# A decoder trunk step on one core: 44 low-part subtractions of dense weights worked out by GpSimd in the odd mixer's first part

## The chip, the cores and the metric

The kernel runs on one core of a Trainium2 chip. Its engines are TensorE (PE; PEld is its weight load), VectorE (DVE), ScalarE (ACT), GpSimd (POOL) and SyncE (SP, which here only issues DMAs). The metric is the device time of one execution in microseconds (us); the median of three executions is given, and one more execution was profiled.

## What is computed

One inference step of a two-layer decoder trunk for 512 prompt tokens and 8 x 4 sample tokens (544 columns in all), with a model width of 1024:

```python
for l in range(DEPTH):                      # DEPTH = 2
    mod = (silu(c) @ ada_w[l] + ada_b[l]).reshape(bx, 3, 3, 1, D_MODEL)
    f = _swiglu(_modulate(x, mod[:, 0]), ffn_w_gate[l, 0], ffn_w_up[l, 0], ffn_w_down[l, 0])
    x = _layer_norm(ALPHA * x + 0.5 * (1.0 + mod[:, 0, 2]) * f, ln_g[l, 0], ln_b[l, 0])
    h = _modulate(x, mod[:, 1])
    m = even_mix(h) if l % 2 == 0 else odd_mix(h)
    x = _layer_norm(ALPHA * x + (1.0 + mod[:, 1, 2]) * m, ln_g[l, 1], ln_b[l, 1])
    f = _swiglu(_modulate(x, mod[:, 2]), ffn_w_gate[l, 1], ffn_w_up[l, 1], ffn_w_down[l, 1])
    x = _layer_norm(ALPHA * x + 0.5 * (1.0 + mod[:, 2, 2]) * f, ln_g[l, 2], ln_b[l, 2])
```

The odd mixer projects h to q, k, v of a dilated attention and to the inputs of RWKV-7 time mixing (`pd = h @ odd_w_in[..., 1536:]`), runs both, and projects their outputs back. RWKV-7 has 8 heads of 64; its state goes from token to token as `s = s*w - (s@kk) x (kk*a) + v x k`.

## The kernel before

**Dense products.** Activations lie with the model dimension on the partitions; a half is 272 of the 544 columns. Every float32 product is made of three float32r products on PE: a weight is split into a high part `wh` and a low part `wl`, an activation into `xh` and `xl`, and `mm3` (L456 to L462) adds wh·xh (L460), wh·xl (L461) and wl·xh (L462) in PSUM.

**Weights.** `tile512` (L442 to L450) makes one tile of 128x512 ready. SP loads it into `raw` (3 buffers), ACT copies it to `wh` (L448), and VectorE writes `wl = raw - wh` (L449), all in order on their queues. In the odd mixer `wh` and `wl` have 4 buffers each (`self.wide(4, 0)`). A strip is two such tiles and serves one block of 128 outputs: 8 steps for each of the two halves, so 48 matmuls, each tile read in both halves. `strip`, `piece` and `proj` call `tile512`.

**The odd mixer's first part** is the code in `odd_mix` from L1681 to L1721. It makes the two strips of the low-rank inputs (`rw_lora`), then the four strips of v (`vproj`), and then, for p = 0 to 3 (two heads each), the generator `rw_first(p)` with three strips (`xmix` of k, r and v), interleaved with `odd_qk(0)` to `odd_qk(2)` (two strips each), `rw_inverse(p)`, the recurrence `rw_rec(0)` and `rw_sample(p)`. `odd_qk(3)` comes later, in the second part. Most of the elementwise work of `rw_first` is VectorE's: L1387 to L1410 prepare k, kk and r, L1402 (`rKBf`) feeds the products of L1422, and L1440/L1441 are 62 small instructions, each of which needs the one before, that solve a triangular system in `rU` (`rEA` comes back through a DMA). L1367 is a scan over the decays. GpSimd makes border columns (L1300, L1301), keeps copies (L1317, L1318 `dsh`; L1448 `rRR`; L1457, L1458), makes small products for the sample (L1396 to L1411 `rSM`) and the diagonal `rMT` (L1449), each behind a wait for ACT or VectorE.

**Order.** The program is written in a rough order; the tile scheduler lays instructions out on each engine by its own estimate of times, and each engine then works strictly in that order. Whatever changes the estimate of one instruction can change the order around it on all engines.

Of the kernel before, what the change touches and what calls it, by code (L numbers as in the profile page):

```python
# [9 lines left out]
F32 = mybir.dt.float32  # L10
# [3 lines left out]
ALU = mybir.AluOpType  # L14
# [12 lines left out]
class Kern:  # L27
    def __init__(self, tc, D, es):
        self.tc, self.nc, self.D, self.es = tc, tc.nc, D, es
        self.n = 0  # L30
        pool = lambda n, b, **k: es.enter_context(tc.tile_pool(name=n, bufs=b, **k))
        self.cp = pool("const", 1)
        self.big = pool("big", 1)
        self.rawp = pool("raw", 3)
        self.sc2 = pool("sc2", 2)
        self.dr = pool("dr", 1, space=DRAM)
        self.banks = ExitStack()
        self.wes = ExitStack()
        self.psum(mm=4, ps=4)
        self.wide()  # L40
        self.xhl = self.xh, self.xl = [self.big.tile([128, 8, NT], F32R, name=n) for n in ("xh", "xl")]
        self.open_x()
# [399 lines left out]
    def tile512(self, src, room=None, lo=None):  # L442
        nc = self.nc
        w = src.shape[1]
        r = self.rawp.tile([128, 512], F32, name="raw")
        nc.sync.dma_start(r[:, 0:w], src)
        wh, wl = (room(n) if room else self.wp.tile([128, 512], F32R, name=n) for n in ("wh", "wl"))
        nc.scalar.activation(wh[:, 0:w], r[:, 0:w], AF.Copy)  # L448
        (lo or nc.vector).tensor_tensor(wl[:, 0:w], r[:, 0:w], wh[:, 0:w].bitcast(F32), op=ALU.subtract)  # L449
        return wh, wl  # L450

    def strip(self, src):
# [1217 lines left out]
    def odd_mix(self):  # L1670
        nc, D, tc = self.nc, self.D, self.tc
        es, ea = ExitStack(), ExitStack()
        pool = lambda n, b, e=es, **k: e.enter_context(tc.tile_pool(name=n, bufs=b, reuse_waits="tile", **k))
        self.wide(4, 0)
        self.psum(mm=2, ps=2, rs=2, rx=1, ro=1)
        self.rob = self.dr.tile([128, 2, SP], F32, name="rob")
        with es:
            pL, self.rg = pool("rkl", 1), pool("rg", 1)
            a1, r0 = pool("oa1", 1), pool("rr", 1)
            self.r0 = r0  # L1680
            self.rsm = pool("rsm", 1)  # L1681
            pA = pool("rk", 1, ea)
            self.rg2 = pool("rgb", 1, ea)
            pJ, p2 = pool("rkj", 1, ea), pool("rk2", 2, ea)
            self.omu = pA.tile([128, 14], F32, name="omu")
            nc.vector.tensor_scalar(self.omu, self.mu, -1.0, 1.0, op0=ALU.mult, op1=ALU.add)
            self.rw_setup(pL, pA, pool("rke", 9, ea), p2, pJ)
            pQ = pool("oqk", 1, side="right")
            self.rw_lora()
            early = {}  # L1690
            for s, k in zip(range(1), ('rx',)):
                src = D["odd_v"][s].rearrange("p k n -> p (k n)")
                w = [self.tile512(src[:, o:o + 512], lambda n: self.rp[0].tile([128, 512], F32R, name=n, tag="e"), None) for o in (0, 512)]
                early[s] = self.proj(None, 0, w, bank=lambda: self.bank[k].tile([128, 512], F32, name=k))
            self.f = {}
            f = [self.rw_first(p) for p in range(4)]
            self.vt = a1.tile([128, 5, 512], F32, name="vt")
            for _ in self.vproj(self.vt, D["odd_v"], self.E, lambda: self.bank["ro"].tile([128, 512], F32, name="ro"), early):
                pass
            nc.sync.dma_start(D["c_v"][0:512].rearrange("(t p) n -> p t n", p=128), self.vt[:, 0:4])  # L1700
            nc.sync.dma_start(D["c_v"][512:544], self.vt[0:32, 4])
            self.qs = a1.tile([128, 4, 32], F32, name="qs")
            self.ks = a1.tile([128, 4, 32], F32, name="ks")
            self.qk = {}
            next(f[0])
            next(f[0])
            for p in range(4):
                if p < 3:
                    next(f[p + 1])
                next(f[p], None)  # L1710
                if p < 3:
                    next(f[p + 1])
                for h in ((0,), (1,), (), (2,))[p]:
                    self.odd_qk(h, pQ)
                self.rw_inverse(p, *self.f[p])
                if p == 1:
                    self.rw_rec(0, r0, p2)
                if p < 3:
                    self.rw_sample(p)
            nc.sync.dma_start(D["d_shift"], self.dsh)  # L1720
            ea.close()  # L1721
            self.psum(mm=1, sc=4, sm=1, rx=1, ro=1)
            a1, pE, a2 = pool("oa3", 1), pool("rre", 2), pool("oa2", 2)
            for n, d in (("dmask", "dmask"), ("mold", "dmold"), ("smask", "dmnew")):
                setattr(self, n, self._ld(a1, d))
            self.qz = a1.tile([128, 3, 2, 128], F32, name="qz")
            nc.gpsimd.memset(self.qz, 0.0)
            pR = pool("ar2", 1)
            self.tmp = pool("art", 2)
            ada = self.ada([(1, 14), (1, 16)], lambda dt, tag: pR.tile([128, 512], dt, name="ar", tag=tag[0] + tag[2:]), lambda: self.bank["mm"].tile([128, 512], F32, name="mm"), 1)  # L1730
            self.rp = (pE, a2)
            self.aoT = a1.tile([128, 4, SP], F32, name="aoT")
            self.ro1 = a1.tile([128, 2, SP], F32, name="ro1")
            self.rw_rec(1, r0, a2)
            self.rw_sample(3, "sm")
            for h in (3,):
                self.odd_qk(h, a1)

            def units():
                for hp in range(4):  # L1740
                    for i in range(4):
                        yield self.odd_head(hp, i, a2)
                        if 4 * hp + i >= 8:
                            for _ in range(2):
                                next(ada, None)
                for _ in ada:
                    pass
            self.ahead(units())
            self.odd_sample(a1, a2)
            for hp in range(4):  # L1750
                self.split(self.xh[:, hp, 0:SP], self.xl[:, hp, 0:SP], self.aoT[:, hp])
            self.split(self.xh[:, 6:8, 0:SP], self.xl[:, 6:8, 0:SP], self.ro1)
            t = a1.tile([128, 2, SP], F32, name="rl", tag="sq")
            nc.sync.dma_start(t, self.rob)
            self.split(self.xh[:, 4:6, 0:SP], self.xl[:, 4:6, 0:SP], t)
            self.rw_sample_end()
        self.psum(mm=4, ps=4)
        self.wide()
# [261 lines left out]
```

## Time and profile before

| | |
|---|---|
| median of three executions | 2573.84 us (2569.62, 2573.84, 2588.95) |
| profiled execution | 2567.64 us, its span 2565.8 us, mean granted clock 0.969 |
| PE busy | 2442.6 us (95%), 20338 matmuls |
| PEld busy | 2253.4 us (88%) |
| DVE busy | 1232.4 us (48%), of these L449 `wl` 458.8 us in 664 |
| ACT busy | 943.3 us (37%), of these L448 `wh` 401.5 us in 664 |
| POOL busy | 409.0 us (16%) |
| chain that ended last, by engine | PE 82%, DVE 7%, DMA 4%, ACT 4%, issue 1%, POOL 1% |

Matmuls are pipelined, so PE's busy time says little about its rate. The granted clock is a share of full speed: 1.00 is 2.4 GHz and 0.50 is 1.2 GHz. The first part of the odd mixer lies between about 1646 and 1885 us of the span. The chain is followed back from the last instruction: at each step it goes to what released it, or to the instruction before it on its engine.

### The profile page before, as it was taken

To read this page: it belongs to the slowest core of one execution; us is meant where nothing else is said; L and a number is where in the kernel's file an instruction comes from. 1 tells how busy PE (TensorE), PEld (TensorE's weight loads), DVE (VectorE), ACT (ScalarE), POOL (GpSimd) and SP (SyncE) were. 2 spreads that over 40 slices of the span, in tenths; PEclk is the share of its full clock that TensorE was granted. 3 is DMA by queue.
4 is the path that set the end of the run, shared out by engine and by line. 5 is a ranking of instruction groups with operands and counts; after the bars stand their busy time and mean duration, and the time that the engine had idled before them with its cause. 6 is when DMAs were issued, how large, how long until landed. Compare 5 with 4: busy or idle time off the path is not lost.

```text
span 2565.8 us, 50682 instructions
## 1 busy us (share of the span) xinstructions
PE 2442.6 (95%) x20338; PEld 2253.4 (88%) x20338; DVE 1232.4 (48%) x2999; ACT 943.3 (37%) x2051; POOL 409.0 (16%) x616
## 2 busy tenths in 40 slices
PE   6999999899899999999999999889999999999996
PEld 4988999897588999999989999878877578999996
DVE  6532356544577333345423334558664567333343
ACT  4322323435555333224323322545422545333222
POOL 1000016411432000031000003312111122000032
PEclk8999999999999999999999999889988999999998
DMA  7666335567632222223562232322322632222221
GB/s 237 203 217 216 113 118 112 188 216 252 222 122 75 87 88 94 80 80 105 173 222 83 85 91 81 103 77 78 92 75 92 211 113 74 87 89 94 80 80 58
DMA packets 184027, 318.27 MB, mean 124 GB/s; under 512 B 38416, under 2 KB 47040, under 8 KB 183664
## 3 DMA queue, kind: packets, MB, share of 16 engines
q1 hardware_dynamic: 172096, 282.52, 34.6%
q0 software_dynamic: 10400, 31.06, 4.1%
q8 instruction: 159, 2.61, 0.4%
q10 hardware_dynamic: 1296, 1.46, 0.2%
q14 instruction: 76, 0.62, 0.1%
HBM read 288.68 MB, written 26.28 MB: 123 GB/s over the span
## 4 chain that ended last, share of the span: by engine, by line
PE 82%; DVE 7%; DMA 4%; ACT 4%; issue 1%; POOL 1%; SPq 1%; ACTq 0%; POOLq 0%; DVEq 0%
PE mm L460 23%; PE mm L462 23%; PE mm L461 22%; PE ps L185 2%; DVE x L347 1%; DMA ar<-in_ada_w 1%; DMA raw<-in_ada_w 1%; ACT t L249 1%; DVE wl L449 1%; PE sc L1178 1%; PE sc L1156 1%; PE ad L185 1%; PE ps L460 1%; PE ps L462 1%; PE ps L461 1%
## 5 line engine op out<-in xcount | busy, mean ns | idle before, releaser
L460 PE MATMUL mm<-xh,wh 128*128 128x272 f32 x3720 | 1089.4, 295 | 35.5 <-ACT xh L250 10.1
L461 PE MATMUL mm<-xl,wh 128*128 128x272 f32 x3720 | 1082.7, 291 | 2.0 <-DVE xl L251 2.0
L462 PE MATMUL mm<-xh,wl 128*128 128x272 f32 x3720 | 1083.0, 292 | 0.8 <-DVE wl L449 0.8
L460 PEld LDWEIGHTS mm<-xh,wh 128*128 128x128 f32 x3720 | 706.0, 190 | 85.2 <-ACT t L401 31.2
L449 DVE TENSOR_TENSOR wl<-raw,wh 128x512 fp32r<-128x512 f32 (+1 forms) x664 | 458.8, 703 | 537.0 <-ACT wh L448 505.0
L461 PEld LDWEIGHTS mm<-xl,wh 128*128 128x128 f32 x3720 | 710.5, 191 | 7.0 <-DVE xl L251 2.5
L462 PEld LDWEIGHTS mm<-xh,wl 128*128 128x128 f32 x3720 | 706.6, 190 | 7.8 <-issue 4.2
L448 ACT ACTIVATE wh<-raw 128x512 fp32r<-128x512 f32 (+1 forms) x664 | 401.5, 618 | 727.6 <-PE mm L461 565.9
L460 PE MATMUL mm<-hh,wh 128*128 128x272 f32 x1280 | 370.4, 289 | 0.0
L462 PE MATMUL mm<-hh,wl 128*128 128x272 f32 x1280 | 370.4, 289 | 0.0
L461 PE MATMUL mm<-hl,wh 128*128 128x272 f32 x1280 | 369.5, 289 | 0.0
L460 PEld LDWEIGHTS mm<-hh,wh 128*128 128x128 f32 x1280 | 241.4, 189 | 0.8 <-issue 0.4
L461 PEld LDWEIGHTS mm<-hl,wh 128*128 128x128 f32 x1280 | 241.2, 188 | 0.4
L462 PEld LDWEIGHTS mm<-hh,wl 128*128 128x128 f32 x1280 | 241.1, 188 | 0.4
L402 DVE TENSOR_TENSOR t<-t,mm 128x272 f32<-128x272 f32 x169 | 73.4, 434 | 279.6 <-ACT t L401 279.4
L401 ACT ACTIVATE t<-mm 128x272 f32<-128x272 f32 x169 | 65.6, 388 | 318.6 <-PE mm L462 318.6
L297 POOL TENSOR_TENSOR sa<-x 128x272 f32<-128x272 f32 x24 | 26.1, 1087 | 907.4 <-DVE x L291 852.0
L291 DVE SCALAR_TENSOR_TENSOR x<-mm,rg,x 128x272 f32<-128x272 f32 (+1 forms) x96 | 45.9, 479 | 171.4 <-PE mm L462 170.7
L466 DVE TENSOR_TENSOR hl<-t,hh 128x272 fp32r<-128x272 f32 x160 | 69.6, 439 | 35.8 <-ACT hh L465 35.3
L465 ACT ACTIVATE hh<-t 128x272 fp32r<-128x272 f32 x160 | 67.5, 426 | 38.5 <-DVE t L402 38.5
L277 POOL TENSOR_TENSOR sq<-sq,t 128x272 f32<-128x272 f32 x60 | 54.7, 926 | 18.1 <-ACT t L276 17.3
L249 ACT ACTIVATE t<-x,S,G 128x272 f32<-128x272 f32 (+1 forms) x80 | 44.5, 589 | 24.1 <-DVE x L348 23.5
(643 smaller groups left out, 2536.6 us busy)
## 6 DMA issues: line engine op xcount, KB each, us to landing
raw<-in_ada_w SPq DMA_DIRECT2D x192, 256.0 KB
raw<-in_wg SPq DMA_DIRECT2D x176, 256.0 KB
raw<-in_wu SPq DMA_DIRECT2D x176, 256.0 KB
raw<-in_wd SPq DMA_DIRECT2D x160, 256.0 KB
ar<-in_ada_w SPq DMA_DIRECT2D x96, 256.0 KB
raw<-in_odd_rw SPq DMA_DIRECT2D x28, 256.0 KB
xs<-x POOLq DMA_DIRECT2D x16, 272.0 KB, 4.0
x<-xs POOLq DMA_DIRECT2D x8, 544.0 KB, 7.8
```

The source lines that it names most:

```text
L185: return nc.tensor.matmul(ps[32 * j:32 * j + 32], self.c32[:, 9 * k:9 * k + 32], r, start=(k == 0), stop=(k == 7))
L249: nc.scalar.activation(t[:, 0:n], x[:, d, c0:pe], AF.Identity, scale=G[:, d, 0:1], bias=S[:, d, 0:1])
L277: G.tensor_tensor(s["q"], s["q"], t, op=A)
L401: self.act = nc.scalar.activation(s, pss[2 * i], AF.Silu)
L402: mul = nc.vector.tensor_tensor(s, s, pss[2 * i + 1], op=ALU.mult)
L448: nc.scalar.activation(wh[:, 0:w], r[:, 0:w], AF.Copy)
L449: (lo or nc.vector).tensor_tensor(wl[:, 0:w], r[:, 0:w], wh[:, 0:w].bitcast(F32), op=ALU.subtract)
L460: nc.tensor.matmul(ps, wh[:, s], mh, start=first, stop=False)
L461: nc.tensor.matmul(ps, wh[:, s], ml, start=False, stop=False)
L462: self.last = nc.tensor.matmul(ps, wl[:, s], mh, start=False, stop=last)
L465: self.nc.scalar.activation(hi, src, AF.Copy)
L466: return (lo_eng or self.nc.vector).tensor_tensor(lo, src, hi.bitcast(F32), op=ALU.subtract)
```

## The change

A field `self.lo` names the engine for the low parts when the caller names none. It is GpSimd from just behind `rw_lora()` to the end of the first part of `odd_mix`, and empty elsewhere. Strips made in between (4 of v, 12 of k, r and v of the time mixing, 6 of q and k: 22 strips, 44 tiles) get their `wl` from GpSimd.

```diff
+        self.lo = None
@@ tile512
-        (lo or nc.vector).tensor_tensor(wl[:, 0:w], r[:, 0:w], wh[:, 0:w].bitcast(F32), op=ALU.subtract)
+        (lo or self.lo or nc.vector).tensor_tensor(wl[:, 0:w], r[:, 0:w], wh[:, 0:w].bitcast(F32), op=ALU.subtract)
@@ odd_mix
             self.rw_lora()
+            self.lo = nc.gpsimd
@@ odd_mix
                 if p < 3:
                     self.rw_sample(p)
+            self.lo = None
             nc.sync.dma_start(D["d_shift"], self.dsh)
```

Lines of the changed kernel stand one to three further down (L449 is L450 there, L1402 is L1403). VectorE has 2957 instructions in place of 3001, GpSimd 665 in place of 621; the other engines have as many as before, in a partly different order from the odd mixer on.

VectorE, the end of `rw_first(0)`'s second piece (`rKBf` goes to PE's L1422; `e` are scratch rows of k and r). Before:

```order
L1397 TENSOR_TENSOR e<-e 128x544
L1398 TENSOR_TENSOR rKBf<-e 128x16x32
L1400 TENSOR_SCALAR e<-e,c_rw_par 128x544
L1406 SCALAR_TENSOR_TENSOR rSM<-rSM,rDC 128x32
L449 TENSOR_TENSOR wl<-raw,wh 128x512
L1401 SCALAR_TENSOR_TENSOR e<-e 128x544
L449 TENSOR_TENSOR wl<-raw,wh 128x512
L1402 TENSOR_TENSOR rKBf<-e 128x16x32
L1409 SCALAR_TENSOR_TENSOR e<-e,c_rw_par 128x544
```

The same place on VectorE now:

```order
L1398 TENSOR_TENSOR e<-e 128x544
L1399 TENSOR_TENSOR rKBf<-e 128x16x32
L1401 TENSOR_SCALAR e<-e,c_rw_par 128x544
L1407 SCALAR_TENSOR_TENSOR rSM<-rSM,rDC 128x32
L1402 SCALAR_TENSOR_TENSOR e<-e 128x544
L1403 TENSOR_TENSOR rKBf<-e 128x16x32
L1410 SCALAR_TENSOR_TENSOR e<-e,c_rw_par 128x544
```

The two subtractions are gone from between k's last steps. GpSimd, the same piece (`rSM` are the sample's small products, each waiting for a VectorE row above). Before:

```order
L1448 COPY rRR<-rQR 128x512
L1396 TENSOR_TENSOR rSM<-e 128x32
L1399 TENSOR_TENSOR rSM<-e 128x32
L1403 TENSOR_TENSOR rSM<-e 128x32
L1405 TENSOR_TENSOR rSM<-rSM,rDC 128x32
L1372 MEMSET e 128x16
```

GpSimd at that place now:

```order
L1449 COPY rRR<-rQR 128x512
L1397 TENSOR_TENSOR rSM<-e 128x32
L1400 TENSOR_TENSOR rSM<-e 128x32
L450 TENSOR_TENSOR wl<-raw,wh 128x512
L1404 TENSOR_TENSOR rSM<-e 128x32
L450 TENSOR_TENSOR wl<-raw,wh 128x512
L1406 TENSOR_TENSOR rSM<-rSM,rDC 128x32
L1373 MEMSET e 128x16
```

Both subtractions stand behind products that wait for VectorE; the second also behind L1404, which waits for VectorE's L1402. VectorE, the head of the triangular solve of p = 1 (the scan is p = 2's). Before:

```order
L1454 TENSOR_TENSOR rKBf<-rKBf,rDC 128x1024
L449 TENSOR_TENSOR wl<-raw,wh 128x512 x2
L1367 SCALAR_TENSOR_TENSOR e<-c_rscan,e 128x544
L1440 TENSOR_TENSOR rtm<-rU,rEA 128x31
L1441 TENSOR_TENSOR rU<-rU,rtm 128x31
```

Now the head is followed by the solve and a part of `rw_inverse(0)` (L1502), and the scan stands further down:

```order
L1441 TENSOR_TENSOR rtm<-rU,rEA 128x60
L1442 TENSOR_TENSOR rU<-rU,rtm 128x3x20
L1441 TENSOR_TENSOR rtm<-rU,rEA 128x76
L1502 TENSOR_TENSOR rVU<-rVU,rs 128x2x128
L1368 SCALAR_TENSOR_TENSOR e<-c_rscan,e 128x544
L1442 TENSOR_TENSOR rU<-rU,rtm 128x4x19
```

The scan of p = 2 moved behind the 13th product of the solve of p = 1.

## Rows read from the trace of the kernel before

**Rows 1.** Busy time by stretch: start:end, length, PE, PEld, DVE, ACT, POOL, granted clock, DMA.
```profile
1646.00:1690.00 44.00, 44.00 (x325) 42.33 (x324) 17.52 (x32) 23.59 (x50) 7.46 (x22) 0.95 0.36 119
1690.00:1730.00 40.00, 29.61 (x215) 26.62 (x214) 25.80 (x63) 17.83 (x31) 9.53 (x22) 0.74 0.20 58
1730.00:1790.00 60.00, 57.16 (x775) 52.68 (x773) 50.74 (x151) 31.85 (x67) 15.08 (x37) 1.00 0.29 81
1790.00:1840.00 50.00, 48.17 (x658) 42.09 (x657) 35.25 (x114) 21.49 (x47) 6.40 (x18) 0.97 0.36 99
1840.00:1885.00 45.00, 43.35 (x729) 36.31 (x731) 23.20 (x56) 12.36 (x30) 10.24 (x16) 0.97 0.18 56
```

**Rows 2.** Waits of PE, 1646 to 1885 us: total us, times, longest.
```profile
PE mm L460 <- ACT pdb L1310: 9.4, 4, 5.2
PE rs L1519 <- DVE rMT L1517: 3.1, 3, 1.6
PE ps L1422 <- DVE rKBf L1402: 2.0, 1, 2.0
PE rs L1528 <- DVE rRR L1526: 2.0, 2, 1.8
```

**Rows 3.** Line L449, 1646 to 1900 us: durations in ns (min/median/max); its waiters.
```profile
L449 DVE TENSOR_TENSOR wl<-raw,wh x44: 667/692/1126, 1647.7 to 1875.1; 128x512 fp32r<-128x512 f32 x44
...
  PEld rs L1615: 0.2, 1
```

**Rows 4.** Groups of instructions on DVE, 1690 to 1885 us: busy us, mean ns, idle before.
```profile
L449 DVE TENSOR_TENSOR wl<-raw,wh 128x512 fp32r<-128x512 f32 x30 | 21.1, 704 | 11.7 <-ACT wh L448 11.7
```

**Rows 5.** The chain that ended last: every piece of L449 in 1690 to 1885 us.
```profile
1706.72 0.71 DVE wl L449
...
1768.19 0.69 DVE wl L449
...
1782.94 0.67 DVE wl L449
...
1814.99 0.68 DVE wl L449
...
1817.62 0.69 DVE wl L449
```

**Rows 6.** Groups of instructions on POOL, 1646 to 1885 us, shapes apart.
```profile
L1449 POOL TENSOR_TENSOR rMT<-rid,rDC 128x1024 f32<-128x1024 f32 x4 | 7.6, 1901 | 14.2 <-PE rx L1544 14.1
L1644 POOL TENSOR_TENSOR rum<-rsw,c_rbmt 128x512 f32<-128x512 f32 x2 | 2.6, 1294 | 4.8 <-DVE rsw L1638 4.8
L1648 POOL TENSOR_TENSOR rS<-rS,rDC 128x512 f32<-128x512 f32 x2 | 2.1, 1044 | 6.9 <-PE rs L1633 6.9
```

**Rows 7.** Timeline of POOL at three places: start, us.
```profile
1717.71 1.90 POOL L1449 TENSOR_TENSOR rMT<-rid,rDC 128x1024 f32<-128x1024 f32 x1
...
1741.52 2.00 POOL L1411 TENSOR_TENSOR rSM<-e 128x32 f32<-128x32 f32 x1 [1.70 <-DVE e L1320]
...
1806.73 1.55 POOL L1644 TENSOR_TENSOR rum<-rsw,c_rbmt 128x512 f32<-128x512 f32 x1 [2.97 <-DVE rsw L1638]
```

**Rows 8.** Timeline of DVE at the same places, and the scan of p = 2.
```profile
1718.48 1.18 DVE L1440 TENSOR_TENSOR rtm<-rU,rEA 128x31 f32<-128x31 f32 x1 [3.13 <-DMA rEA<-rab]
...
1719.92 0.19 DVE L1440 TENSOR_TENSOR rtm<-rU,rEA 128x30 f32<-128x30 f32 x1
...
1758.51 1.29 DVE L1367 TENSOR_TENSOR_SCAN e<-c_rscan,e 128x544 f32<-128x544 f32 x1 [1.84 <-ACT e L1354]
...
1782.13 0.75 DVE L1395 TENSOR_TENSOR rQR<-e 128x512 f32<-128x512 f32 x1
...
1807.70 1.13 DVE L449 TENSOR_TENSOR wl<-raw,wh 128x512 fp32r<-128x512 f32 x1 [0.32 <-ACT wh L448]
```

**Rows 9.** Waits of ACT, 1646 to 1885 us: the longest in total.
```profile
ACT wh L448 <- PE mm L461: 46.5, 29, 9.9
```

**Rows 10.** Waits of SP's queue, 1646 to 1885 us: the longest in total.
```profile
SPq L446 <- DVE wl L449: 92.5, 26, 15.4
```

## Prediction

> **What bounds the kernel now.** I read the page first: PE is busy 95% of the span and holds 82% of the chain that ended last, so a VectorE instruction counts only where PE stands still. Next I split the mixer's first part into stretches [rows 1]. From 1646 to 1690 us PE has no idle time at all. From 1690 to 1885 it is idle 40 - 29.61 + 60 - 57.16 + 50 - 48.17 + 45 - 43.35 = 16.7 us of 195, most of it before 1730, where the granted clock also falls to a mean of 0.74 (PE runs part of that stretch at 1.2 GHz). VectorE is busy 25.80 + 50.74 + 35.25 + 23.20 = 135.0 us of those 195, and most densely from 1730 to 1790, with 50.74 of 60. GpSimd is busy under 50 us in all five stretches together.
>
> Then I asked what PE waits for there [rows 2]: 9.4 us for PSUM banks that ACT has not emptied, and 2 to 3.1 us each for three VectorE results (rMT, rKBf, rRR). A low part is not among them. The view of the line itself says the same: 44 subtractions with a median of 0.692 us, and only 0.2 us of PEld's waits are put down to them [rows 3]. So wl is always early, and its only way to the end is that it stands in VectorE's queue ahead of results that PE does wait for. The chain shows how often: 5 of the 30 that lie behind 1690 us are on it, with 0.71 + 0.69 + 0.67 + 0.68 + 0.69 = 3.4 us [rows 4, 5].
>
> **What goes.** 14 of the 44 lie before 1690 us, where PE is never idle: nothing to gain. The other 30 take 21.1 us off VectorE [rows 4], and 3.4 us off the chain [rows 5]: a sixth (3.4/21.1 = 0.16) of what is taken off the engine counts at the end.
>
> **What comes.** The trace has no subtraction of raw and wh on GpSimd, and no GpSimd result in float32r. The nearest rows are its float32 products of two 128x512 inputs: L1648 with 1.044 us, and L1644 with a mean of 1.294 [rows 6], one of which took 1.55 [rows 7]. I take 1.04 for one that is left alone, since shape and number of inputs agree, and keep 1.55 as the upper end. GpSimd gets 44 x 1.04 = 46 us of work (68 at the upper end) in 239 us, beside the 48.7 it has: 40 to 49% busy, so it does not become the bound.
>
> But the two engines get in each other's way. At 1717.71 GpSimd began the 1.90 us of L1449, up to 1719.61 [rows 7]; VectorE's L1440, which takes 0.19 us, began at 1718.48 and took 1.18, up to 1719.66 [rows 8]. VectorE stood until GpSimd had ended. At 1806.73 both had two inputs to read: L1644 took 1.55 in place of 1.04, and the VectorE subtraction behind took 1.13 in place of 0.69 [rows 7, 8]. At 1741.52 GpSimd waited instead: 2.00 us for a 128x32 product, under four VectorE instructions in a row [rows 7]. The Trainium skill (SBUF — State Buffer, Who interferes with whom) says that a VectorE instruction with two SBUF inputs and a GpSimd instruction that reads SBUF share one read interface, and that the second to come is blocked until the first ends; the first two places agree with it, with 1.18 us where 0.19 would do. It speaks against this change; what it would do is the first rival.
>
> So a subtraction on GpSimd is free for VectorE only where VectorE has nothing to do. Without wl, VectorE works 135.0 - 21.1 = 113.9 of 195 us, a share of 0.58. The 30 hold the inputs for 30 x 1.04 = 31.3 us; of these 0.58, or 18.3 us, fall on VectorE's other work and push it back. VectorE thus gets 21.1 - 18.3 = 2.8 us in all. Between the ends (no hold falls on it: 21.1 gained; all do: 31.3 - 21.1 = 10.2 lost) I take the share of busy time, since nothing aligns the two queues. At the end a sixth counts: 18.3 x 0.16 = 3.0 us come, 3.4 go, **net -0.4 us**.
>
> The Trainium skill (GPSIMD Engine Reference, Performance versus the Vector engine) gives GpSimd 1.96 times VectorE's time for such an addition. An estimate by it is 0.692 x 1.96 = 1.36 us for each, and the same sum then gives +0.4 us instead of -0.4; L1648's 1.044 us is only 1.5 times 0.692, and the sum goes by that.
>
> **Is wl late for PE?** By rows 1 a matmul of the stretch before 1690 takes 44.00/325 = 0.135 us, so a strip of 48 lasts 6.5 us. There are four buffers, two strips; the first tile of a strip is free after three quarters of it and is read again at the start of the strip after the next, 1.25 strips or 8.1 us later, and for the second tile it is the same. ACT's copy begins as soon as the buffer is free: it waits 46.5 us for exactly that [rows 9]. With a microsecond each for copy and subtraction some 6 us are left. On GpSimd the subtraction takes up to 0.9 us longer, and ahead of it may stand a 1.90 us L1449 or a product that waits for VectorE by a microsecond or two: 3 to 5 us at worst. I cost it at nothing; the cover is about 6 us, and a tile that used it all up would cost PE the rest. Behind a waiting L450 on GpSimd stand copies and sample products that PE does not wait for in these rows [rows 2]. SP's raw loads wait for wl (92.5 us in 26 waits [rows 10]) and would be issued up to 0.9 us later; the three raw buffers reach 1.5 strips ahead, 9.8 us, so this costs nothing either.
>
> **What else moves.** The scan of p = 2 stood in a gap of VectorE at 1758.51 and now stands behind the 13th product of a solve. It comes some 5 us later (12 pairs, each instruction 0.19 us [rows 8] or a little more); its results are first used on VectorE at 1782.13 [rows 8], 22 us behind its end, so the delay is covered, and the 1.29 us now lie in dense work: at most +1.3, by the sixth 0.2. The number of ACT's table loads is unchanged.
>
> **The rivals.**
> - **The lock decides (slower).** Where VectorE is densest, every hold falls on it, the two never fit together, and VectorE is the engine that PE waits for. Price: 10.2 us if all of the loss reaches the end, and 30 x 1.55 - 21.1 = 25 us if the holds are also 1.55 long. It turns slower once over 21.1/31.3 = 67% of the holds fall on VectorE work; from 1730 to 1790 its busy share is 85% now, and that speaks for it. Against it: PE has other work queued while VectorE is late, and only a sixth counted so far. Profiled time 2571 to 2578. This is also where the skill's rule leads if it holds without exception.
> - **VectorE's relief counts in full (faster).** The two subtractions at 1705 and 1706.72 go from in front of rKBf, for which PE waits 2.0 us [rows 2], in the stretch with the low clock. Then 3.4 us go and nothing comes back, a sixth of the 11.7 us that VectorE stood waiting for wh [rows 4] is 1.9 more, and if PE's clock stays up for a third of the stretch (29.61 x 0.26/3 = 2.6 us) it is 8 us: 2560. Against it: GpSimd's subtraction is ready at the same moment, and rKBf's inputs have to wait for it.
> - **Low parts come late for PE.** GpSimd's queue stands behind a wait while PE reaches the tile. Each such tile costs the lateness beyond 6 us; 30 tiles with 1 us each would be +30, 2598. No wait of GpSimd in the new order leads back to the strip itself, so I hold it unlikely.
> - That the change moves nothing is out: VectorE loses 44 instructions and GpSimd gains 44.
>
> **How the numbers follow.** The sum is 2567.64 - 0.4 = 2567.2 us for the profiled execution. The median of the three runs shown is 6.2 us above that execution; the two lower runs are 2.0 and 6.2 above it, 4.1 on average, and I add 4.1: **2571 us**. Chances: this sum, within 4 us either way, 0.50; the lock 0.24; full relief 0.20; late low parts 0.04; the rest, a changed order with an effect of its own, 0.02. The range goes from 2560 (full relief, 2560, which as a run lies 0 to 4 us above it) to 2585 (the lock's 10.2, 2578, with the median's 6.2), and leaves out late low parts, the longest holds and half of the extremes. A measurement of this kernel tells about 1% (26 us) from no change: faster 0.02, within 1% 0.93, slower 0.05.
>
> **What would show it.** Right: L450 at 1.04 to 1.6 us on GpSimd; PE's waits on L463 (wl) still under a microsecond; VectorE's busy time from 1690 to 1885 within some 5 us of before, since stretched instructions make up for the 30 that left; L1441 or L1442 with single rows of about 1.2 us beside a subtraction; the last L450 within 4 us of 1875 us, where the last moved subtraction starts now [rows 3]. Wrong: a subtraction of 2 us or more (the float32r result is slow there), PE waits on L463 of several us, or VectorE's solve stretched so that rMT or rRR waits of PE grow by 10 us.

## The result, and the profile after

The changed kernel takes 2599.76 us (median of six runs, 2592.95 to 2602.65) where the kernel before takes 2575.62 (six runs, 2569.62 to 2588.95). The two medians are 24 us apart. The ratio on record is an estimate of its own, not the quotient of these medians: 1.0070, with a 95% interval of 1.0052 to 1.0088, **some 18 us slower**, where 2571 and no change had been forecast. Two more comparisons of the same two kernels on other chips gave 1.0050 (1.0035 to 1.0066) and 1.0056 (1.0043 to 1.0070), some 13 and 14 us. The profiled execution took 2592.95 us, its span 2591.1, mean granted clock 0.964 (before 2567.64, 2565.8 and 0.969).

Not all of the 25 us between the two spans is the change's. Some 6 to 9 us arise at 640 to 720 us, in the even mixer, where the two programs are the same; the experiments below show such differences there between kernels with an equal program (560 to 720 us: granted clock 0.96 in one profile of the kernel before, 0.88 in another kernel that is no slower than it). The median of the kernel before is also not the same on every chip, 2568.9 to 2582.4. So runs are compared by their ratio to the kernel before on the same chip, and profiles by what PE does from a given matmul on.

The profile after, busy time by stretch, the columns as in [rows 1]:

```profile
1646.00:1690.00 44.00, 35.90 (x263) 34.26 (x263) 14.79 (x38) 23.38 (x52) 22.28 (x34) 0.92 0.36 119
1690.00:1730.00 40.00, 29.10 (x231) 25.23 (x230) 20.67 (x32) 22.26 (x40) 20.80 (x31) 0.84 0.32 98
1730.00:1790.00 60.00, 53.14 (x536) 49.22 (x536) 45.44 (x137) 25.17 (x55) 21.14 (x37) 0.88 0.23 63
1790.00:1840.00 50.00, 48.01 (x634) 42.65 (x635) 29.75 (x65) 19.86 (x43) 19.02 (x35) 0.97 0.33 95
1840.00:1885.00 45.00, 41.92 (x614) 36.54 (x612) 30.05 (x98) 20.81 (x45) 11.62 (x23) 0.92 0.20 54
```

The row to look at is 1730 to 1790: PE ran 775 matmuls there in [rows 1] and was busy for 57.16 us at a granted clock of 1.00. Now it gets 536 done, is busy for 53.14, and the clock has a mean of 0.88. (The first row begins earlier in the program than in [rows 1], because of the 9 us.) PE's waits behind 1690 us, from the waits of PE of 1646 to 1885 us (total us, times, longest), which answer [rows 2]:

```profile
PE rs L1520 <- DVE rMT L1518: 3.0, 1, 3.0
PE ps L1423 <- DVE rKBf L1403: 3.0, 1, 3.0
PE rs L1499 <- DVE rVU L1502: 2.0, 2, 1.5
...
PE ps L1471 <- DVE e L1463: 1.4, 1, 1.4
PE rs L1529 <- DVE rRR L1527: 1.1, 1, 1.1
PE rs L1515 <- DVE rVU L1502: 1.0, 2, 0.5
```

PE is idle for 22.8 us behind 1690 us, where it was 16.7. New are rVU (L1502, the subtraction of `rw_inverse`) and `e` (L1463), 4.4 us together. Of the old ones, rMT has a longer single wait, 3.0 where it was 1.6. The 3.0 of rKBf tells nothing: a second profile of the kernel before has 3.0 as well. The moved line itself, 1646 to 1900 us (durations in ns, min/median/max; no waiter is listed for it):

```profile
L450 POOL TENSOR_TENSOR wl<-raw,wh x44: 1259/1278/1752, 1656.7 to 1899.4; 128x512 fp32r<-128x512 f32 x44
```

### The profile page after: what moved, and what is told of

Same layout as the page of the kernel before. It is cut to its first block, busy times and chain, and to the rows that moved or that the text cites. A ratio compares the mean times of both kernels' runs of the same rounds, so it can differ in the third digit from the quotient of the medians.

```text
span 2591.1 us, 50665 instructions
## 1 busy us (share of the span) xinstructions
PE 2458.6 (95%) x20338; PEld 2262.1 (87%) x20338; DVE 1223.9 (47%) x2955; ACT 943.6 (36%) x2051; POOL 457.2 (18%) x660
## 5 line engine op out<-in xcount | busy, mean ns | idle before, releaser
L450 DVE TENSOR_TENSOR wl<-raw,wh 128x512 fp32r<-128x512 f32 x620 | 427.5, 702 | 514.1 <-ACT wh L449 480.1
L449 ACT ACTIVATE wh<-raw 128x512 fp32r<-128x512 f32 (+1 forms) x664 | 401.3, 618 | 722.7 <-PE mm L462 554.1
L450 POOL TENSOR_TENSOR wl<-raw,wh 128x512 fp32r<-128x512 f32 x44 | 57.5, 1313 | 88.0 <-ACT wh L449 78.9
```

Of the source, the lines that this page charges most:

```text
L450: (lo or self.lo or nc.vector).tensor_tensor(wl[:, 0:w], r[:, 0:w], wh[:, 0:w].bitcast(F32), op=ALU.subtract)
```

## Experiments

Two causes are possible. **The hold**: GpSimd's subtractions delay VectorE. **The order**: the scheduler laid the instructions of all engines out differently. Issue-order edges tell them apart. They fix which instruction of an engine is issued ahead of which, and add no wait between engines. A kernel with such edges carries a table of places in the written program, and behind the program:

```python
def pin(nc, tc):
    ins = list(nc.cur_bb.bb.instructions)
    for steps in json.loads(zlib.decompress(base64.b85decode(ORDER))):   # one list per engine
        at = steps[0]
        for d in steps[1:]:
            tc.add_manual_dep(ins[at + d], ins[at].name, DependencyInfo(NoSync, DATA), reason="order")
            at += d
```

"Old order" means that every instruction but the 44 low parts stands on its engine as in the kernel before; "new order", as in the changed kernel. The places of the 44 themselves are the scheduler's in either. "Zeros" is the run that writes zeros in place of the subtraction.

### Hold and order, each alone

`pool_oldorder` is the changed kernel in the old order:

```diff
         with ExitStack() as es:
             Kern(tc, D, es).run()
+        pin(nc, tc)        # ORDER: the order before the change
```

> The changed kernel (44 low parts on GpSimd), with every engine's other instructions pinned by issue-order edges to the order that they had before the change; only the place of the 44 in GpSimd's queue is the scheduler's. Theory A (the new order costs the time: the scan of p = 2 and rw_inverse(0) changed places): ratio to before 0.998 to 1.002, since the order that costs is gone; profiled span near 2566. Theory B (the hold: GpSimd's 1.28 us subtractions push VectorE's dense chains back and lower PE's clock): the loss stays, ratio 1.005 to 1.009, L1441 rows of 1.2 us beside subtractions. Theory C (most of the difference is execution to execution, the first 9 us of it in the even mixer): ratio 1.000 to 1.004, and the lag against before at 720 us of the span anywhere from 0 to 9.

Measured: 1.0041 (1.0027 to 1.0055), 10.5 us. **The hold alone costs 0.4%.**

`dve_neworder` is the kernel before with the same two lines, and ORDER from the changed kernel:

> The kernel before (all low parts on VectorE), with every engine's other instructions pinned to the order of the changed kernel. Theory A (order): slower like the changed kernel, ratio 1.005 to 1.009, and VectorE stands some 9 us for rEA at about 1776 us. Theory B (hold): no loss, ratio 0.998 to 1.002. If order and hold each cost a part, this one and the run with the old order share the 18 us between them.

Measured: 1.0050 (1.0036 to 1.0064), 12.9 us. **The order alone costs 0.5%**, without one low part moved. Neither theory is out; each alone is nearly as slow as the changed kernel.

`pool_memset` writes zeros in place of the subtraction, in the old order:

```diff
-        (lo or self.lo or nc.vector).tensor_tensor(wl[:, 0:w], r[:, 0:w], wh[:, 0:w].bitcast(F32), op=ALU.subtract)
+        self.lo.memset(wl[:, 0:w].bitcast(F32), 0.0) if self.lo else (lo or nc.vector).tensor_tensor(...)
```

> Old order pinned, and in place of each of the 44 subtractions GpSimd writes zeros to the same tile of 128x512: the low part of these weights is left out of the result. VectorE is relieved of 44 instructions, GpSimd has as many, but they read no SBUF. Theory B (the hold by reading): faster than or equal to before, 0.995 to 1.000 (3.4 us of the chain gone, nothing back), and no L1441 row of 1.2 us beside a memset. Theory A: the same, 0.998 to 1.000, since the order is the old one. If it is as slow as the changed kernel, neither the reading nor the order is the cause but GpSimd's writes or the missing VectorE rows themselves.

Measured: 0.9998 (0.9989 to 1.0007). VectorE is busy for 1206.1 us in place of 1232.4, and no gain is seen. **The loss does not come with the move as such, but with what a subtraction does and zeros don't**: it reads, and takes longer. A relief of less than 2.8 us (0.11%) would not show in this ratio, and the profiles speak for one. From the first matmul of L1353 (L1354 here) to the end of the span the kernel before takes 906.5 and 905.2 us in its two profiles, and this one 902.4 in its only one. That is 2.8 to 4.1 us less, about the 3.4 that were forecast to go. So the relief is small, and whether it is nothing or some 3 us stays open.

`before_again` is the kernel before, profiled once more.

> The kernel before, unchanged, profiled once more. Theory C: its span differs from 2565.8 us by up to 9 us, and part of it lies at 665 to 705 us, in the even mixer, where the program is the same in all kernels here. Theories A and B: within 3 us of 2565.8, and no shift at 665 to 705 us.

Its span was 2565.3 us, 0.5 from the first, with up to 4.1 us between the two on the way (at 701 us). The row of busy time by stretch of this kernel in the even mixer and, on another chip, of `pool_off_solve` (below), which is no slower than the kernel before:

```profile
560.00:720.00 160.00, 152.13 (x1132) 109.07 (x1133) 79.06 (x256) 86.38 (x210) 47.07 (x79) 0.96 0.69 219
```

```profile
560.00:720.00 160.00, 151.16 (x1065) 109.14 (x1064) 72.40 (x229) 73.41 (x181) 39.58 (x70) 0.88 0.66 212
```

In equal programs PE has 67 matmuls fewer done here, at a clock of 0.88 in place of 0.96. That part of the 25 us is not the change's.

### What a hold looks like

The old order makes rows comparable one by one. Timeline of VectorE under zeros (start, us, [idle before]):

```profile
1729.65 0.72 DVE L1388 TENSOR_TENSOR e<-e 128x544 f32<-128x544 f32 x1 [1.39 <-ACT e L1386]
1730.29 0.22 DVE L1442 TENSOR_TENSOR rU<-rU,rtm 128x68 f32<-128x68 f32 x1
1730.43 0.72 DVE L1389 SCALAR_TENSOR_TENSOR e<-e 128x544 f32<-128x544 f32 x1
```

The same three in `pool_oldorder`:

```profile
1732.02 0.73 DVE L1388 TENSOR_TENSOR e<-e 128x544 f32<-128x544 f32 x1 [1.39 <-ACT e L1386]
1732.66 1.30 DVE L1442 TENSOR_TENSOR rU<-rU,rtm 128x68 f32<-128x68 f32 x1
1733.89 1.82 DVE L1389 SCALAR_TENSOR_TENSOR e<-e 128x544 f32<-128x544 f32 x1
```

and GpSimd's timeline beside them:

```profile
1732.59 2.54 POOL L450 TENSOR_TENSOR wl<-raw,wh 128x512 fp32r<-128x512 f32 x2 [7.82 <-ACT wh L449]
```

L1442 begins just behind the first of two subtractions and ends as it ends (1732.66 + 1.30 = 1733.96, the subtraction 1732.59 + 2.54/2 = 1733.86); L1389 begins beside the second and ends 0.6 us behind it (1735.71 and 1735.13). VectorE loses 2.2 us at this place. The sum over the kernel is in VectorE's busy time on the page, with the same 2955 instructions each time. Zeros, then whole subtractions:

```profile
PE 2445.8 (95%) x20338; PEld 2254.5 (88%) x20338; DVE 1206.1 (47%) x2955; ACT 943.5 (37%) x2051; POOL 424.4 (17%) x660
```

```profile
PE 2448.4 (95%) x20338; PEld 2256.7 (88%) x20338; DVE 1223.1 (47%) x2955; ACT 944.2 (37%) x2051; POOL 459.2 (18%) x660
```

1223.1 - 1206.1 = **17.0 us of holds**; GpSimd's subtractions are 58 us long together, so 29% of their time comes back as longer VectorE work. The Trainium skill (SBUF — State Buffer, Who interferes with whom) says that the second to come on the shared read interface is blocked until the first ends; the rows at 1732.66 agree with it, and the zeros, which read nothing, hold nobody here: no VectorE row of L1442 is longer than 0.28 us under zeros, and the longest in `pool_oldorder` has 1.31. Nor does any wait of PE or VectorE from 1690 to 1890 us in `pool_oldorder` end with a result of GpSimd, so it is not GpSimd's own results that come too late.

### Where a hold counts

`pool_on_solve` gives GpSimd only the 20 low parts that stood beside the triangular solves, `pool_off_solve` only the other 24, both in the old order:

```diff
+        self.nlo += bool(self.lo)
-        (lo or self.lo or nc.vector).tensor_tensor(wl[:, 0:w], ...)
+        (lo or self.lo if 18 < self.nlo <= 38 else nc.vector).tensor_tensor(wl[:, 0:w], ...)
```

> Old order pinned; only the 20 low parts (19th to 38th) that GpSimd worked out beside the triangular solves (1732 to 1839 us in the run with the old order) are GpSimd's, the other 24 VectorE's. If what counts is a hold in the solve, where each instruction needs the one before: all of the 0.4% stays, 1.0035 to 1.0045. If every hold counts alike: 20 of 44, 1.0015 to 1.0025.

> The complement: the 24 low parts away from the solves on GpSimd, the 20 beside them on VectorE, old order pinned. If holds count in the solve alone: 0.999 to 1.001. If every hold counts alike: 1.002 to 1.003. If relief is worth anything outside the solves, below 0.999, and this one would be faster than both kernels.

Measured: 1.0038 (1.0022 to 1.0054) beside the solves, 0.9997 (0.9983 to 1.0011) away from them. **The hold's cost comes from the 20 beside the solves; the other 24 cost nothing that is seen.** Nor is a gain seen from them, though one of less than 4.4 us would not show in this ratio; by the count above (from L1354 to the end of the span) the profile of the 24 has 903.5 us, 1.7 to 3.0 less than the kernel before. VectorE's busy time says the same of the holds. Each low part that leaves VectorE takes (1232.4 - 1206.1)/44 = 0.60 us off it (less than its own 0.69, since neighbours overlap). Without holds it would be 1232.4 - 20 x 0.60 = 1220.4 and 1232.4 - 24 x 0.60 = 1218.0; it is 1235.2 and 1218.9, so 14.8 us of holds beside the solves and 0.9 elsewhere. The waits of PE from the second L1423 of p = 1 on, 1766 to 1860 us. `pool_off_solve`:

```profile
PE rs L1520 <- DVE rMT L1518: 2.2, 2, 2.0
PE rs L1529 <- DVE rRR L1527: 2.0, 2, 1.8
```

`pool_on_solve`:

```profile
PE rs L1499 <- DVE rVU L1502: 5.0, 1, 5.0
PE rs L1520 <- DVE rMT L1518: 3.6, 2, 3.4
PE rs L1529 <- DVE rRR L1527: 2.1, 1, 2.1
```

The 5.0 us are a chain. The timeline of VectorE in `pool_off_solve` and then in `pool_on_solve`:

```profile
1778.68 0.20 DVE L1441 TENSOR_TENSOR rtm<-rU,rEA 128x31 f32<-128x31 f32 x1 [3.39 <-DMA rEA<-rab]
...
1780.86 0.41 DVE L1502 TENSOR_TENSOR rVU<-rVU,rs 128x256 f32<-128x256 f32 x1
```

```profile
1782.37 0.19 DVE L1441 TENSOR_TENSOR rtm<-rU,rEA 128x31 f32<-128x31 f32 x1 [6.83 <-DMA rEA<-rab]
...
1786.57 0.41 DVE L1502 TENSOR_TENSOR rVU<-rVU,rs 128x256 f32<-128x256 f32 x1
```

The holds in the solve of p = 0 make rMQ late, with it the transfer that brings rEA, and so the head of the solve of p = 1, for which VectorE stands 6.83 us in place of 3.39. Counted from the L1423 at 1766 us, the head is 3.5 us later; 2.0 of them are there when SP issues the transfer (1775.28 and 1773.10), the rest is added while the transfer runs, which no hold explains. Behind that head, ten instructions further, L1502 is queued, for which PE waits. Between head and L1502 two more holds of a microsecond follow (4.20 us in place of 2.18). Then the clock goes. Busy time by stretch from the same matmul on, 20 us each, `pool_off_solve`:

```profile
1766.30:1786.30 20.00, 20.00 (x206) 17.69 (x206) 12.54 (x41) 13.11 (x26) 1.91 (x9) 1.00 0.46 117
1786.30:1806.30 20.00, 17.57 (x341) 16.14 (x340) 18.56 (x60) 9.85 (x21) 4.09 (x10) 1.00 0.10 32
1806.30:1826.30 20.00, 20.00 (x262) 17.29 (x262) 13.36 (x31) 5.07 (x14) 5.15 (x9) 1.00 0.43 106
```

and `pool_on_solve`:

```profile
1766.49:1786.49 20.00, 15.52 (x149) 13.47 (x149) 9.35 (x27) 11.91 (x23) 6.49 (x11) 0.94 0.45 111
1786.49:1806.49 20.00, 19.45 (x307) 18.35 (x308) 15.86 (x53) 8.44 (x17) 3.59 (x7) 0.80 0.08 27
1806.49:1826.49 20.00, 17.91 (x275) 15.91 (x276) 13.88 (x41) 5.96 (x15) 7.91 (x16) 0.88 0.34 85
```

PE is idle 4.48 us in the first stretch, 0 in the other kernel. In the second, when it is busy again, the granted clock has a mean of 0.80 in place of 1.00: 20 x 0.20 = up to 4.0 us at full speed, on top of the wait. Stretches of 10 us of `pool_on_solve` show that the clock is back at 1.00 before it falls once more (PE alone: busy, granted clock, DMA):

```profile
1790.00:1800.00 10.00, 10.00 (x151) 0.78 0.01 2
1800.00:1810.00 10.00, 8.10 (x150) 1.00 0.19 55
1810.00:1820.00 10.00, 9.81 (x117) 0.83 0.13 21
```

The second fall, which makes the 0.88 of the third stretch, stands behind the wait of 2.1 us for rRR at 1808 and comes only after the clock had recovered from the first; in `pool_off_solve` a wait of 1.8 us for rRR leaves the clock at 1.00.

`pool_both`: VectorE keeps its 44 and GpSimd reads as well (old order).

```diff
-        (lo or self.lo or nc.vector).tensor_tensor(wl[:, 0:w], ...)
+        (lo or nc.vector).tensor_tensor(wl[:, 0:w], ...); self.lo and self.lo.tensor_tensor(self.dup, wh..., wh..., op=ALU.subtract)
```

> Old order pinned, VectorE keeps its 44 low parts, and GpSimd in addition subtracts wh from itself into a scratch tile 44 times (bf16 result, read by nobody): the hold without the relief. The runs so far say that the relief is worth nothing (zeros from GpSimd: ratio 0.9998) and the hold 0.4% (old order: 1.0041). If that holds, the ratio is 1.004 again, and VectorE has some 20 instructions of 1.2 us where 0.2 would do. If relief is worth the 3.4 us that the chain showed, this one is slower than the old order by that: 1.0055. If the hold needs the wait for a result of GpSimd, 1.000.

Measured: 1.0056 (1.0034 to 1.0078). The hold needs no result of GpSimd. Against 1.0041 the intervals overlap, so this run can't say what the relief is worth.

### Shorter holds

`pool_copy` lets GpSimd copy raw (one input); `pool_halves` works each low part out in two halves of 256 columns; both in the old order.

```diff
-        (lo or self.lo or nc.vector).tensor_tensor(wl[:, 0:w], ...)
+        self.lo.tensor_copy(wl[:, 0:w], r[:, 0:w]) if self.lo else (lo or nc.vector).tensor_tensor(wl[:, 0:w], ...)
```

```diff
-        (lo or self.lo or nc.vector).tensor_tensor(wl[:, 0:w], ...)
+        [(lo or self.lo or nc.vector).tensor_tensor(wl[:, a:z], ...) for a, z in (((0, 256), (256, w)) if self.lo else ((0, w),))]
```

> Old order pinned; GpSimd copies raw to the low part's tile (one input of 128x512 in place of two; the low part of these weights is wrong by that, and counts as the weight itself). If any GpSimd instruction that reads SBUF holds VectorE's two-input instructions: rows of L1441 and L1442 as long as what is left of the copy, and a loss in proportion to its length; 1.002 to 1.004 if it takes 0.5 to 1.3 us. If only a two-input instruction holds: 1.000, as with the zeros.

> Old order pinned, 44 low parts on GpSimd, each worked out in two halves of 256 columns: 88 instructions of about 0.65 us. A VectorE instruction is then held for half as long, but twice as often. If the total of the holds decides: 1.003 to 1.005, as with whole tiles (1.0041 and 18 us stretched). If single long holds decide, as the one-input copy of 0.61 us suggests (4.9 us stretched, ratio 0.9994): 0.999 to 1.002.

| in the old order | one on GpSimd, median | VectorE busy | holds | ratio to before |
|---|---|---|---|---|
| zeros, 44 | 0.526 us | 1206.1 | 0 | 0.9998 (0.9989 to 1.0007) |
| copy, 44 | 0.612 us | 1211.5 | 5.4 | 0.9994 (0.9982 to 1.0006) |
| halves, 88 | 0.734 us | 1220.9 | 14.8 | 1.0028 (1.0014 to 1.0041) |
| whole, 44 | 1.282 us | 1223.1 | 17.0 | 1.0041 (1.0027 to 1.0055) |

(Holds are VectorE's busy time less that under zeros.) No cost is seen for 5.4 us; 14.8 cost 7, 17.0 cost 10.5, each net of what the relief is worth. Two halves are longer than one whole (1.47 us) and stretch more of VectorE's rows, each by less, so their total is hardly smaller. Whether single length or total decides is not told apart by this. The cost is hardly proportional to the total (5.4 us would then cost 3.3, and the interval of the copies ends at 1.5), but three points whose intervals in part overlap give no more than that.

### What in the order costs

`pool_lora_first` is the changed kernel with five edges in place of the table: on PE, ACT and VectorE p = 2's decays (L1354, their sigmoids, the scan) ahead of rw_inverse(0).

```diff
+EDGES = ((17154, 16930), (17156, 16950), (17155, 16938), (17157, 16958), (17158, 16939))
```

> The changed kernel with five issue-order edges only: on PE, ACT and VectorE the decays of p = 2 (the products of L1354, their sigmoids, the scan of L1368) stand ahead of rw_inverse(0)'s instructions, as before the change; all else is the scheduler's. If the order's cost (12.9 us, ratio 1.0050 with the low parts on VectorE) comes from p = 2 starting behind rw_inverse(0): ratio about 1.004, as with the whole old order pinned. If it lies in the rest of the new order: 1.007, as the changed kernel.

Measured: 1.0075 (1.0053 to 1.0096). My first theory of the order, that p = 2's decays start too late, gains nothing from it. It isn't a clean test: with these decays ahead ACT has one ACT_TABLE_LOAD more (1.28 us; 2052 instructions on the page in place of 2051), in this kernel and in the four below that share its order of the decays. Three runs followed on one chip: the same order with the low parts on VectorE, the changed kernel once more, and the new order with four steps of rw_inverse(0) later on PE. The edit of the last, in PE's list (mm3 are dense matmuls):

```diff
 mm3 x37
+L1353 x2, mm3 x14
 L1498 x16
-L1353 x2, mm3 x14
+L1353 x2, mm3 x14
 L1498 x16
-L1353 x2, mm3 x14
+mm3 x24
 L1514 x32
-mm3 x24
+mm3 x20
 L1519 x32
-mm3 x20
```

> All low parts on VectorE, every engine's other instructions pinned to the order of the run with the five edges (decays of p = 2 ahead of rw_inverse(0); with the low parts on GpSimd it was 1.0075). If that order is no better than the changed kernel's: 1.003 to 1.006, and PE waits of 1 to 3 us at 1760 to 1785 us with a granted clock under 1 behind them. If that order is as good as the old one and GpSimd's holds alone made its 1.0075: 0.999 to 1.001.

> The changed kernel, unchanged, beside the others on one chip. Ratio again 1.005 to 1.009; the two parts measured alone (hold 1.0041, order 1.0050) add up to 1.009, so 1.007 would say that they share a part of their waits.

> All low parts on VectorE, the changed kernel's order pinned, but on PE four steps of rw_inverse(0) (both groups of L1498, L1514, L1519) stand one piece of 14 to 24 dense matmuls later each. If the order costs because PE reaches these steps before rTT and rMT are there (1.61 and 3.13 us of waits at 1761 and 1779) and its clock falls behind the waits (0.69 and 0.83 in the two stretches of 10 us), both are gone: 1.000 to 1.002. If the order costs by something else (the later p = 2 itself): still 1.004 to 1.006.

Measured: 1.0060 (1.0042 to 1.0077), 1.0050 (1.0035 to 1.0066) and 1.0041 (1.0027 to 1.0055). The covered steps no longer wait, but PE then waits 2.3 us for ACT's decays, 1.9 for pdb and 1.9 for L1382: the waits have moved. Then the scan was put into VectorE's wait for rEA: with the low parts on VectorE by VectorE's list, and with them on GpSimd by its edge, which now leads to the head of the solve (five edges again, where the expectation says six).

```diff
 L1454
+L1367
 L1440, L1441: the first 11 of the solve of p = 1
-L1367
```

```diff
-(17158, 16939)
+(17158, 17241)
```

The third is the first of these two with the old order as VectorE's list:

```diff
-ORDER = [PE, DVE, ACT, POOL, SP] of dve_scan_gap
+ORDER = [PE, ACT, POOL, SP] of dve_scan_gap, [DVE] of the kernel before
```

> As the run with that order and the low parts on VectorE (1.0060), but the scan of p = 2 stands ahead of the first product of the solve of p = 1, in the 5.3 us that VectorE stood there for rEA, in place of behind its 11th. If the order costs because the scan lies inside the solve (1.28 us in the solve, and all of p = 2 five to seven us later): most of the loss goes, 1.000 to 1.003. If it lies elsewhere in the new order: 1.005 to 1.007 again.

> The changed kernel (44 low parts on GpSimd, the scheduler's own order) with six issue-order edges: the decays of p = 2 ahead of rw_inverse(0) on PE, ACT and VectorE, and the scan ahead of the solve of p = 1. If the scan's place is what the order costs: as the old order with GpSimd's holds, 1.003 to 1.005. If not: 1.006 to 1.008, as with five edges (1.0075).

> PE, ACT, GpSimd and SP in the order of the run before (scan of p = 2 in the gap, 1.0051), the low parts on VectorE, but VectorE's other instructions in the order before the change. There rw_inverse(0)'s four subtractions stand behind the 10th, 11th, 19th and 22nd instruction of the solve of p = 1 (18th, 19th, 36th and 39th in the run before), its two rMT behind the 35th (50th, 51st), and p = 2's elementwise steps between the 36th and 50th (51st to the end). If VectorE's order is what the new order costs: 1.000 to 1.002, and PE's waits of 1.50 and 2.15 us at 1786 to 1794 us are gone. If it is the order of the matmuls: 1.004 to 1.006 again.

Measured: 1.0051 (1.0033 to 1.0068), 1.0043 (1.0031 to 1.0055) and 1.0067 (1.0053 to 1.0081). With the low parts on GpSimd, the scan in its gap gives what was expected if the scan's place were all that the order costs: 1.0043 in place of 1.0075 on another chip, no more than the hold alone. With them on VectorE it gives what was expected if the cost lies elsewhere: 1.0051 in place of 1.0060, with no hold of GpSimd to explain the rest. So the scan's place can be a part of the cost, and it isn't all of it; nor does VectorE's old order alone bring the time back. What these orders have in common is seen in the 50 us from the second L1422 (L1423) of p = 1 on, the row of busy time by stretch. The kernel before, `before_again`:

```profile
1751.23:1801.23 50.00, 47.57 (x701) 42.31 (x702) 37.30 (x116) 25.90 (x55) 7.92 (x25) 1.00 0.32 82
```

`dve_neworder`, then `dve_scan_gap`, then `dve_old_vector`:

```profile
1755.00:1805.00 50.00, 44.98 (x579) 40.59 (x580) 34.03 (x105) 22.33 (x47) 5.88 (x19) 0.90 0.28 72
```

```profile
1770.20:1820.20 50.00, 45.68 (x632) 41.07 (x636) 33.90 (x107) 24.95 (x50) 6.59 (x20) 0.93 0.31 79
```

```profile
1753.61:1803.61 50.00, 44.62 (x581) 40.70 (x581) 34.93 (x115) 24.39 (x49) 6.28 (x20) 0.93 0.23 57
```

The old order keeps PE busy for 47.57 us at a clock of 1.00 and gets 701 matmuls done. Each of the three other orders shown has 1.9 to 3 us more of idle time and a clock of 0.90 to 0.93, and 69 to 122 matmuls fewer. Where PE waits differs each time: rTT (1.6) and rMT (3.1) in `dve_neworder`, rVU (1.5) and L1514 (2.2) in `dve_scan_gap`, rVU (2.6) and rRR (2.8) in `dve_old_vector`. That the waits go with the order is shown; **which row of the new order starts them is not settled**, and with the low parts on VectorE the old order is the only one of those tried that keeps the stretch full.

### Do hold and order add up?

The changed kernel and its order alone, on one chip:

> The changed kernel once more, on one chip with the next: 1.005 to 1.007.

> The changed kernel's order with all low parts on VectorE, once more, beside the changed kernel itself. If the hold adds its own 10 us to the order's: 1.001 to 1.003 where the changed kernel has 1.005 to 1.007. If the two share their waits (the order alone was 1.0050): equal to the changed kernel within 0.15%.

Measured: 1.0056 (1.0043 to 1.0070) and 1.0048 (1.0034 to 1.0062). On top of the new order the 44 moved subtractions cost 0.08%, which this measurement can't tell from nothing. In the changed kernel, then, the loss is the order's (12 to 13 us). The hold would cost about as much by itself; a likely reason why it adds nothing here, not shown by a run, is that it falls into a stretch in which VectorE and PE already wait.

## Why the prediction was wrong

- **What bounds the kernel: right.** PE is the bound, VectorE counts where PE waits, and wl is never late. The rival of late low parts (+30 us) is out: L450 on GpSimd has no waiter, although it takes nearly twice as long.
- **The price: mis-sized.** I took 1.04 us from the product L1648 [rows 6]; the subtraction takes 1.278 (median in the changed kernel), between that row and the upper end of 1.55. That is 1.278/0.692 = 1.85 times VectorE's time. The Trainium skill (GPSIMD Engine Reference, Performance versus the Vector engine) has 1.96; the estimate from it, 1.36, was nearer than the row that I chose.
- **The holds: right in size, by luck.** 18.3 us were forecast from 30 subtractions of 31.3 us together, a share of 0.58. In the old order it was 17.0, from 44 of 58 us together, a share of 0.29. Longer subtractions and a smaller share of them on VectorE's work cancel.
- **"At the end a sixth counts": the step that failed for the hold.** The sixth came from the subtractions that stood on the chain [rows 4, 5]. For what is lost it does not hold: 10.5 of 17.0 us counted, not 0.16 of them. Holds fall where VectorE is densest, in the solves, in which every instruction needs the one before and whose end a transfer, the next solve and PE wait for; and behind one wait of 5.0 us PE's clock took up to 4.0 us more. For what is gained the sixth is neither shown nor refuted: 3.4 us were expected, the ratio of the zeros has room for up to 2.8, and their profile is 2.8 to 4.1 shorter. The rival "the lock decides" had the direction and the place (1730 to 1790) right for the hold alone, and I gave it 0.24. That its price of 10.2 us meets the 10.5 is luck: it let all of 31.3 us fall on VectorE and set 21.1 of relief against them, where 17.0 fell on it and the relief was some 3 us at the most. In the changed kernel the hold adds nothing that can be measured, so the lock is not what decided there.
- **"What else moves ... covered": the step that failed for the order, and the one that decides.** I looked at one moved row, the scan of p = 2, and gave the order no cost. I forecast the scan 5 us later. It came 24.6 us later by the clock (1758.51 in [rows 8]), of which 10 are the lag that the program had there anyway:

```profile
1776.14 0.19 DVE L1441 TENSOR_TENSOR rtm<-rU,rEA 128x31 f32<-128x31 f32 x1 [8.93 <-DMA rEA<-rab]
...
1783.10 1.28 DVE L1368 TENSOR_TENSOR_SCAN e<-c_rscan,e 128x544 f32<-128x544 f32 x1
```

  I had counted the 13 products ahead of it, not VectorE's wait for rEA at the head of the solve, which the scan used to fill and now stands behind: 8.93 us there. The cover of 22 us was read wrongly too. It counted VectorE only, but ACT works the decays out of the scan's result at once: at 1760.80 in the kernel before, 1.0 us behind the scan's end. In the changed kernel ACT stands 4.13 us for the scan; what that costs by itself was not measured. ACT's timeline after:

```profile
1784.46 1.28 ACT L1375 ACT_TABLE_LOAD   x1 [4.13 <-DVE e L1368]
```

  But the scan was one row of 228 on VectorE and 1098 on PE that stand elsewhere, and putting it back did not bring all of the time back. What the runs show in place of "covered" is that the order alone costs 0.48% to 0.50% (12 to 13 us), with waits of PE and a clock of 0.90 to 0.93 in 50 us that were nearly full before; which row starts them stays open. A changed order with an effect of its own had a chance of 0.02 and no price.
- **The range.** It ended at 2585, which is the lock's 10.2 us and the median's 6.2; the order had no price that could widen it. With holds at 10.5 and an order at 12.9 us, 2580 to 2600 would have been the case to cover. The bound of 1% was not what such a comparison can tell either; the intervals here reach 0.09% to 0.22% to each side.
- **Faster than both.** No version was found. Leaving the subtractions out bounds what moving them could bring in this order: with zeros it is 0.9998, 2.8 us faster at the most; the 24 away from the solves are at 0.9997.

## What to carry to other kernels

Taking work off an engine that is not the bound is worth what the bound waits for it; test that first by leaving the work out in an unchanged order. When a scheduler lays the program out anew, the new order is a change of its own: pin the old one, and measure the edit and the order apart. Before work goes to GpSimd, look at what VectorE does at that moment: here a dependent chain of 0.2 us instructions beside a reader of 1.3 us is where nearly all of the holds fell, and where they cost.

## What the runs showed of the hardware

- A two-input subtraction of 128x512 with a float32r result takes GpSimd 1.28 us, more than its float32 product of that shape [rows 6]; 128x256 takes 0.734, more than half. A copy with one input takes 0.612, writing zeros 0.526.
- A VectorE instruction of 0.2 us with two inputs takes up to 1.35 beside such a subtraction. Beside one-input copies most of the stretched ones take 0.54 to 0.65 (5.4 us of holds in sum); beside zeros the longest L1442 takes 0.28.
- Behind a wait of PE of 5.0 us (`pool_on_solve`) the granted clock has a mean of 0.80 over the 20 us from 1786 on and is back at 1.00 from 1800 to 1810 us, where the kernel without that wait has 1.00 throughout.
